# A sliding-window copy on one core: SP's copies shifted by two packets per DMA engine, the mends moved to ACT's queue

## The chip, the cores and the metric

The kernel runs on one core of one Trainium2 chip. Nothing is computed on the compute engines; every byte is moved by the core's 16 DMA engines, which take their work from three queues: SP's (q1 in the profile), ACT's (q10) and POOL's (q0). The metric is device time in microseconds (us), the median of several runs; lower is better.

## The reference

The input has 32 batches of 4096 rows of 256 floats. Each batch yields 127 windows of 64 rows, one every 32 rows:

```python
n_windows = (length - window_size) // stride + 1        # (4096 - 64)//32 + 1 = 127
for i in range(n_windows):
    start = i * stride
    result[:, i] = x[:, start:start + window_size].copy()
```

A *block* is 32 rows, 32 KB; a batch has 128 blocks. A *window* is two neighbouring blocks, 64 KB, so every inner block is written twice. The output is 32 x 127 windows, 266 MB.

## The kernel before

**Two ways for a batch.** The odd batches 1, 3, ..., 21 (`STAGED`, eleven of them, numbered n = 0 to 10) go through SBUF: a load of 4 MB puts block p on partition p of one of five tiles, and a store writes each block to its two places, 8 MB in packets of 32 KB. The loads are queued by POOL in packets of 16 KB (load 0 by ACT), the stores by ACT. All other batches go straight from DRAM to DRAM on SP's queue, one packet of 64 KB for each window (`rows`). A DMA of 128 rows gives each of the 16 engines 8 packets, one of 112 rows gives it 7, one of 32 rows 2; an instruction's packets are followed on each engine by a 4-byte packet that reports to the semaphore.

**Overruns and what mends them.** A store writes the halves from one before its batch to one after it, so it spoils the last half window of the batch before and the first half window of the batch behind. `full(b)` copies 128 windows of a batch that has 127, so it spoils window 0 of the next batch. Whatever is spoiled is written again later, and the order of these writes is what the waits guard:

- `EARLY` = 16, 18, 20, 22 are copied whole at the start (semaphore `early`), before the stores of 15 to 21, which wait for them. The halves that those stores spoil are rewritten by the two *mends* (`halves`, 48 and 64 packets of 2 KB), which wait for those stores.
- `ROW` = 24 to 30 are copied whole one after the other: each waits for the one before (`chain`), since each spoils the next one's window 0.
- `BESIDE` = 0, 2, ..., 14: windows 15 to 126 are copied after the store of batch b + 1 has landed; windows 0 to 14 come later, for four batches in one DMA (`firsts`, 60 packets of 64 KB).
- 23 and 31: their windows 15 to 126 come behind the loop (23 in two parts), windows 0 to 14 at the very end (`firsts((23, 31))`, 30 packets), when the copies of 22 and 30 have landed.

**SP's order.** Everything on SP's queue is written out by hand in `copies()` and `ends()`. At the start there are four copies: 48 windows of batch 16 (in packets of 32 KB, L136), its other 80, and two of 64 windows of batch 18. Then the loop over `BESIDE` alternates one whole batch (20, 22, 24, ..., 29: 128 windows) with 112 windows of a `BESIDE` batch. One passage through the loop is 240 packets of 64 KB on SP's queue, and it stands against one store (256 packets of 32 KB) and one load (256 of 16 KB). Behind the loop come `firsts` of 0 to 6, batch 30, then 32 and 80 windows of 23 and 112 of 31, then (after waits for `early`, for `fringe` and for three stores) the mends, `firsts` of 8 to 14 and `firsts` of 23 and 31.

**ACT's order.** Load 0, stores 0 to 9, and the last store in three pieces (`LAST`): blocks 0 to 31, blocks 96 to 127 (both report to `fringe`) and blocks 32 to 95.

**POOL** queues loads 1 to 10, each waiting for the store that frees its tile, and at the end waits for every semaphore. All DMA instructions carry line L84, the helper `start`.

Of the kernel before, what the change touches and what calls it, by code (L numbers as in the profile page):

```python
# [16 lines left out]
EARLY = (16, 18, 20, 22)  # L17
ROW = tuple(range(24, 31))
BESIDE = tuple(range(0, 16, 2))

REST = 15
# [5 lines left out]
class _Geometry:  # L27


    def __init__(self, x, out, W, S):  # L30
        self.B, self.L, self.D = x.shape
        self.x, self.out = x, out
        self.n_win = (self.L - W) // S + 1
        self.n_blk = self.L // S
        self.blk = S * self.D
        self.win = W * self.D
        assert W == 2 * S and self.n_blk == self.n_win + 1 == 128
# [33 lines left out]
class _Kernel:  # L71
    def __init__(self, nc, g, tiles):
        self.nc, self.g, self.tiles = nc, g, tiles
        self.loaded = [nc.alloc_semaphore(f"loaded{i}") for i in range(len(tiles))]
        self.stored = [nc.alloc_semaphore(f"stored{i}") for i in range(len(tiles))]
        self.copied = nc.alloc_semaphore("copied")
        self.chain = nc.alloc_semaphore("chain")
        self.first = nc.alloc_semaphore("first")
        self.early = nc.alloc_semaphore("early")
        self.fringe = nc.alloc_semaphore("fringe")  # L80
        self.count = {}

    def start(self, engine, out, in_, sem, packet=65536):
# [46 lines left out]
    def copies(self):  # L130


        g, nc, n_win = self.g, self.nc, self.g.n_win
        sp = nc.sync

        self.rows(EARLY[0], 0, 48, self.early, COPY_PACKET // 2)  # L136
        self.rows(EARLY[0], 48, 80, self.early)
        self.rows(EARLY[1], 0, 64, self.early)
        self.rows(EARLY[1], 64, 64, self.early)

        whole = EARLY[2:] + ROW
        for n, b in enumerate(BESIDE):
            if whole[n] in ROW[1:]:
                self.all_of(sp, self.chain)
            self.full(whole[n], self.early if whole[n] in EARLY else self.chain)
            self.after_store(sp, STAGED.index(b + 1))
            self.rows(b, REST, n_win - REST, self.copied)

        self.start(sp, *g.firsts(BESIDE[:4]), self.copied)
        self.all_of(sp, self.chain)  # L150
        self.full(ROW[-1], self.chain)
        self.rows(23, REST, 32, self.copied)

    def ends(self):
        g, nc, n_win = self.g, self.nc, self.g.n_win
        sp = nc.sync

        self.rows(23, REST + 32, n_win - REST - 32, self.copied)
        self.rows(31, REST, n_win - REST, self.copied)
        self.all_of(sp, self.early)  # L160
        self.all_of(sp, self.fringe)
        for n, s in enumerate(STAGED[:-1]):
            if s + 1 in EARLY:
                self.after_store(sp, n)
        self.start(sp, *g.halves(EARLY[:3], 2 * n_win - 1, g.n_blk - 1), self.copied)
        self.start(sp, *g.halves(EARLY, 0, 0), self.copied)
        self.start(sp, *g.firsts(BESIDE[4:]), self.copied)
        self.all_of(sp, self.chain)
        self.start(sp, *g.firsts((23, 31)), self.copied)


@with_exitstack
def kernel(
    ctx: ExitStack,
    tc: tile.TileContext,
    x: bass.AP,
    window_size: bass.AP,
    stride: bass.AP,
    out: bass.AP,
):  # L180
    nc = tc.nc
    W, S = int(window_size), int(stride)
    g = _Geometry(x, out, W, S)
    assert 0 not in STAGED and g.B - 1 not in STAGED
    pool = ctx.enter_context(tc.tile_pool(name="blocks", bufs=1))
    tiles = [pool.tile([g.n_blk, g.blk], x.dtype, name=f"xb{i}") for i in range(BUFS)]

    with tc.tile_critical():
        k = _Kernel(nc, g, tiles)
        k.load(0)  # L190
        k.copies()
        for n in range(1, len(STAGED)):
            k.load(n)
        waited = False
        last = len(STAGED) - 1
        for n, s in enumerate(STAGED):
            if not waited and (s - 1 in EARLY or s + 1 in EARLY):
                k.all_of(nc.scalar, k.early)
                waited = True
            if n < last:  # L200
                k.store(n, 0, g.n_blk)
            else:
                for p0, rows in LAST:
                    alone = p0 > 0 and p0 + rows < g.n_blk
                    k.store(n, p0, rows, None if alone else k.fringe)

        k.ends()

        sems = [*k.loaded, *k.stored, k.first, k.early, k.copied, k.chain, k.fringe]
        for sem in sems:  # L210
            k.all_of(nc.gpsimd, sem)
        nc.gpsimd.dma_reset()
        used = sorted(sem.num for sem in sems)
        assert used == list(range(used[0], used[-1] + 1))
        nc.gpsimd.sem_clear(range(used[0], used[-1] + 1))
# [35 lines left out]
```

## Time and profile before

| | |
|---|---|
| median of 3 runs | 766.52 us (763.76 to 766.72) |
| the profiled execution | 766.23 us, of it span 764.5 us |
| moved by the DMA engines | 314.15 MB, mean 411 GB/s |
| read from and written to HBM | 221.87 MB and 268.01 MB, 641 GB/s over the span |
| SP's queue q1 | 175.74 MB |
| ACT's queue q10 | 96.47 MB |
| POOL's queue q0 | 41.94 MB |
| an 8 MB store of ACT, from issue to landing (median) | 102.8 us |
| the mends, from issue to landing | 7.4 us (96 KB) and 11.5 us (128 KB) |
| last instructions of SP's queue issued | 732.82 to 738.45 us |

The three queues' bytes count every packet once; a packet from DRAM to DRAM is read from and written to HBM, a load is only read, a store only written. A queue's *share* in the profile is the time that its packets took, added up over the 16 engines and divided by 16 times the stretch asked for. So share x 16 x stretch / packets is the time of one packet. "Under 512 B" counts mostly the 4-byte reports to semaphores.

### The profile page before, as it was taken

What the parts mean: (1) busy time and instruction counts of PE and PEld (TensorE: products, weight loads), DVE (VectorE), ACT (ScalarE), POOL (GpSimd) and SP (SyncE); (2) the same over time, 40 slices, a digit from 0 to 9 for tenths busy, and PEclk for the clock granted to TensorE, in tenths of its full rate; (3) what the DMA queues carried; (4) which work ended last, traced back from release to release, by engine and by line L of the source; (5) the groups of instructions that cost most, each with busy time, mean ns of one, the idle gap of its engine ahead of it and who ended that gap; (6) DMA issues with size and microseconds to landing.
All of it is one profiled execution on the core that took longest, in us unless ns stands there. A gap on an engine that the chain in (4) does not pass through costs nothing.

```text
span 764.5 us, 116 instructions
## 1 busy us (share of the span) xinstructions
POOL 7.5 (1%) x14
## 2 busy tenths in 40 slices
POOL 1000000000000000000000000000000000000000
DMA  9999999999999999999999999999999999999995
GB/s 375 434 421 410 415 441 413 424 393 436 412 423 420 432 409 413 435 414 430 393 427 422 412 426 426 428 399 424 421 418 425 402 421 413 424 407 394 393 420 192
DMA packets 9187, 314.15 MB, mean 411 GB/s; under 512 B 845, under 2 KB 845, under 8 KB 957
## 3 DMA queue, kind: packets, MB, share of 16 engines
q1 hardware_dynamic: 3299, 175.74, 55.9%
q10 hardware_dynamic: 3168, 96.47, 30.0%
q0 software_dynamic: 2720, 41.94, 13.1%
HBM read 221.87 MB, written 268.01 MB: 641 GB/s over the span
## 4 chain that ended last, share of the span: by engine, by line
another core or an unknown queue 56%; POOL 1%; issue 0%; PEldq 0%
POOL xb L84 1%; PEldq L246 0%
## 5 line engine op out<-in xcount | busy, mean ns | idle before, releaser
L84 POOL DMA_DIRECT2D xb<-in_x_dram x10 | 7.3, 728 | 430.9 <-DMA out_dram<-xb 429.9
L232 POOL MEMSET const-bfloat16-1.0<- 128x1 bf16 x1 | 0.1, 96 | 0.0
L232 POOL MEMSET const-float32-0.0<- 128x1 f32 x1 | 0.1, 93 | 0.2 <-issue 0.2
L232 POOL MEMSET const-uint8-127<- 128x1 uint8 x1 | 0.1, 94 | 0.0
L232 POOL MEMSET const-float32-1.0<- 128x1 f32 x1 | 0.1, 93 | 0.0
## 6 DMA issues: line engine op xcount, KB each, us to landing
out_dram<-xb ACTq DMA_DIRECT2D x10, 8192.0 KB, 102.8
xb<-in_x_dram POOLq DMA_DIRECT2D x10, 4096.0 KB, 236.7
xb<-in_x_dram ACTq DMA_DIRECT2D x1, 4096.0 KB, 23.2
out_dram<-xb ACTq DMA_DIRECT2D x2, 2048.0 KB, 52.7
out_dram<-xb ACTq DMA_DIRECT2D x1, 4096.0 KB, 70.5
out_dram<-in_x_dram SPq DMA_DIRECT2D x1, 3072.0 KB, 23.8
out_dram<-in_x_dram SPq DMA_DIRECT2D x26, 67.6
out_dram<-in_x_dram SPq DMA_DIRECT2D x1, 128.0 KB, 11.5
```

What stands on the lines that cost most here:

```text
L84: engine.dma_start(out=out, in_=in_, max_dma_last_dim=packet).then_inc(sem, 16)
L232: nc = _bacc.Bacc("TRN2", target_bir_lowering=False, num_devices=1)
```

## The change

`copies()` now copies batch 18 in one DMA of 128 windows instead of two of 64, and adds 32 windows of batch 23 (15 to 46) right behind it, ahead of the loop. The loop itself is untouched. Behind it, 23's windows 47 to 78 stand where 15 to 46 stood; then come 31's 112 windows, the last 48 of 23, `firsts` of 8 to 14, the waits for `early` and `chain`, and `firsts` of 23 and 31. SP no longer waits for stores behind the loop, and `ends()` is gone. The two mends, with their waits for `fringe` and for the three stores, are issued by ACT behind its last store (`mends()`), on a semaphore of their own, `mended`.

```diff
-        self.rows(EARLY[1], 0, 64, self.early)
-        self.rows(EARLY[1], 64, 64, self.early)
+        self.full(EARLY[1], self.early)
+        self.rows(23, REST, 32, self.copied)
...
         self.full(ROW[-1], self.chain)
-        self.rows(23, REST, 32, self.copied)
-
-    def ends(self):
-        g, nc, n_win = self.g, self.nc, self.g.n_win
-        sp = nc.sync
-
-        self.rows(23, REST + 32, n_win - REST - 32, self.copied)
+        self.rows(23, REST + 32, 32, self.copied)
+
         self.rows(31, REST, n_win - REST, self.copied)
+        self.rows(23, REST + 64, n_win - REST - 64, self.copied)
+        self.start(sp, *g.firsts(BESIDE[4:]), self.copied)
         self.all_of(sp, self.early)
-        self.all_of(sp, self.fringe)
+        self.all_of(sp, self.chain)
+        self.start(sp, *g.firsts((23, 31)), self.copied)
+
+    def mends(self):
+
+        g, act = self.g, self.nc.scalar
+        self.all_of(act, self.fringe)
         for n, s in enumerate(STAGED[:-1]):
             if s + 1 in EARLY:
-                self.after_store(sp, n)
-        self.start(sp, *g.halves(EARLY[:3], 2 * n_win - 1, g.n_blk - 1), self.copied)
-        self.start(sp, *g.halves(EARLY, 0, 0), self.copied)
-        self.start(sp, *g.firsts(BESIDE[4:]), self.copied)
-        self.all_of(sp, self.chain)
-        self.start(sp, *g.firsts((23, 31)), self.copied)
+                self.after_store(act, n)
+        self.start(act, *g.halves(EARLY[:3], 2 * g.n_win - 1, g.n_blk - 1), self.mended)
+        self.start(act, *g.halves(EARLY, 0, 0), self.mended)
```

More of the change, by code (lines that the diff above doesn't have):

```diff
@@ L80, in __init__ @@
         self.fringe = nc.alloc_semaphore("fringe")
+        self.mended = nc.alloc_semaphore("mended")
         self.count = {}
@@ L205 @@
                     k.store(n, p0, rows, None if alone else k.fringe)
-        k.ends()
-        sems = [*k.loaded, *k.stored, k.first, k.early, k.copied, k.chain, k.fringe]
+        k.mends()
+        sems = [*k.loaded, *k.stored, k.first, k.early, k.copied, k.chain, k.fringe, k.mended]
         for sem in sems:
```

## The prediction

> **What bounds the kernel now.** I read the page first, then the DMA queues in short stretches, then the landings and the single packets of one engine.
>
> ```profile
> DMA  9999999999999999999999999999999999999995
> q1 hardware_dynamic: 3299, 175.74, 55.9%
> q10 hardware_dynamic: 3168, 96.47, 30.0%
> q0 software_dynamic: 2720, 41.94, 13.1%
> ```
>
> The engines are busy throughout: 55.9 + 30.0 + 13.1 = 99.0%. No wait of an instruction sets the end; the sum of packet times does. All that can be won is packets that take less than now and the 1% of idle time (7.6 us) at the two ends. POOL's 430 us of waiting costs nothing.
>
> So: how long is a packet? SP's 64 KB take 55.9% x 764.5 x 16 / (175.74 MB / 65,536) = 2.55 us on average. Three stretches around the end of one store of ACT, which lands at 437.6, in this order: 416 to 428, 428 to 438, 438 to 448 us.
>
> ```profile
> q1 hardware_dynamic: 56, 2.62, 50.5%
> q10 hardware_dynamic: 55, 1.67, 32.2%
> ...
> q1 hardware_dynamic: 37, 2.42, 64.8%
> q10 hardware_dynamic: 38, 0.85, 19.8%
> q0 software_dynamic: 36, 0.59, 15.1%
> ...
> q1 hardware_dynamic: 38, 2.49, 57.5%
> q10 hardware_dynamic: 37, 1.21, 28.1%
> ```
>
> First stretch: 50.5% x 12 x 16 / 40.0 packets = 2.42 us. Second: 64.8% x 160 / 36.9 = 2.81. Third: 57.5% x 160 / 38.0 = 2.42. The middle one is where a store gives way to the next on ACT's queue: q10 falls to 0.85 MB, and SP fills the gap. In the first stretch SP changes from one copy to the next (its share falls to 50.5%), and no packet suffers.
>
> Why that is, one engine's packets between 350 and 372 us show (S = SP 64 KB, A = ACT 32 KB, P = POOL 16 KB, s and a = their semaphore reports of 0.01 us): P s A P S A P S **a** P S A P S. The queues take turns, one packet each, and a report uses up a turn. Where ACT's turn is a report, two S stand with only a P between them: they took 2.42 and then 2.74 us, and the next 3.01. On nearly every engine one of the two S behind a takes 2.7 to 3.8 us. Where SP's turn is a report, A, P, A stand side by side: nothing is slow.
>
> SP's report comes two rounds before ACT's. A passage of SP's loop is 8 + 1 + 7 + 1 = 17 turns; a store is 16 + 1 and a load 16 + 1. All three recur every 17 rounds, so the distance stays: a `BESIDE` copy issued at 437.59 lands 58.3 us later at 495.9, the store issued at 402.94 lands 102.6 later at 505.5, 9.6 us apart; at 301.4 it is 9.1, at 573.6 it is 9.8.
>
> Last, the end: 674 to 728, 732 to 740 and 744 to 756 us.
>
> ```profile
> q1 hardware_dynamic: 264, 14.16, 66.5%
> q10 hardware_dynamic: 265, 7.41, 34.3%
> ...
> q10 hardware_dynamic: 92, 2.75, 79.7%
> q1 hardware_dynamic: 100, 0.60, 21.1%
> ...
> q1 hardware_dynamic: 85, 3.88, 91.7%
> ```
>
> Without POOL the 64 KB take 2.66 us; then ACT runs almost alone beside the 2 KB mends; then SP alone at 2.97 us a packet.
>
> **The change part by part.** *The shift.* Behind the copy of 48 windows SP had 6 + 5 + 5 = 16 turns ahead of the loop (80, 64 and 64 windows, each with a report); now it has 6 + 9 + 3 = 18 (80, 128 and 32). The loop begins two turns later, and SP's report falls into the round of ACT's: S A P **s a** P S A P. No two S have a lone P between them. This holds at every store, since each recurs in 17 turns, if SP's queue never runs dry. It doesn't: a `BESIDE` copy is issued when a store lands (437.59) while a whole batch of some 36 us still stands in the queue, now 8.5 us more of it than before; a whole batch is issued when the one before has landed (464.42), with a `BESIDE` copy of 31 us ahead of it, as before.
>
> *What a store's end costs now.* In the ten us before a landing, each queue's (packet time - 2.42, 1.21 or 0.61) x packets / 16: at 437.6 SP 0.39 x 36.9 / 16 = 0.90, POOL (0.67 - 0.61) x 36 / 16 = 0.13: 1.03 us. The same rows give 0.91, 1.23, 0.91, 1.03, 1.16, 1.00, 1.07, 1.06 and 0.88 for the nine landings from 96 to 642: 9.25 us together. Not all of it comes back as time. SP's old report stretch, free of excess now, becomes an ordinary one: between store ends the excess is 1.18 us in 55.5 (mean of six periods), and as some 11 of these are the free stretch, 0.027 a us, 0.27 for ten us, 2.4 for nine. Shift: -9.25 + 2.4 = -6.8 us. The bounds: nothing, if the excess only moves; -9.25, if the new stretch gives the same relief. I take -6.8, because the relief stretch (2.42 us with SP at its report) and the kernel's start show the packets next to such a round: at 23 to 27 us, with ACT's queue empty and SP's report between two P, P s P S, the S took 2.42.
>
> *The mends.* On SP they are 3 + 4 packets and two reports an engine, in turns with ACT's 32 KB (7.4 and 11.5 us to landing). Their packets total 112 x 0.09 / 16 = 0.65 us. The waits for `fringe` and the stores move to ACT, behind its last instruction: nothing but the mends is queued behind them there, and POOL's final wait, which gets one semaphore more (0.09 us). `fringe` is complete at 732.8, when the last piece of 8 packets an engine is still running, so ACT's queue has no gap.
>
> *The end.* Behind store 9 SP has 8 + 4 + 5 + 3 = 20 turns, ACT 5 + 5 + 9 = 19 and then the mends: both end in about the same round. Compare per engine from the landing of 31 before (726.7 to 736.3, about 731.5), with 6 S and 7 or 8 A left. Before: 7.5 x 1.21 + 0.65 + 6 x 2.93 (746 to 762 us) = 27.3. After, side by side at the packet times of 674 to 732 (2.65 and 1.30): 15.9 + 9.75 + 0.65 = 26.3. -1.0 us. Bounds: +2 (the engines end 6.4 us apart now; the slowest decides, and mends alone at the end may not be hidden) to -3.
>
> *The rest* (one DMA issue fewer at the start, four waits of SP) lies beside busy queues: nothing; if that cover were gone, an issue is 0.5 to 0.9 us.
>
> Sum: 766.2 (profiled execution; 0.3 below the median of 766.5) - 6.8 - 1.0 = 758.4, and 0.3 more against the median: **758.7 us**.
>
> **The rivals.** *The excess only moves (22%).* HBM delivers 641 GB/s over the span, and a period of 68.2 us (store landings 96.0 to 641.9, eight periods) moves 16 x (2 x 15 x 64 + 16 x 32 + 16 x 16 KB) = 44.0 MB, 645 GB/s; without any excess it would be 15 x 2.42 + 16 x 1.21 + 16 x 0.61 = 65.4 us. If memory and not the sequence is the limit, packets elsewhere grow by what the store ends lose, and only the end is won: 765.5. For it: 674 to 732 us, two queues, is slow at every packet. Against it: 416 to 428 and 438 to 448 show 436 and 431 GB/s without excess, and 428 to 438 only 387. The Trainium skill (DMA: Bandwidth & Descriptors, Rules for kernel authors) speaks for this rival: spreading DMAs over SP, ACT and GpSimd doesn't help bandwidth, as they interleave on the same 16 engines. By that rule the sum would be that of the rival or 766.5; the trace's 2.42 against 2.81 us speaks against it, as far as it is read to mean that the order of interleaving is free.
>
> *Both queues restart together (12%, slower).* In the shared round an engine has only two 16 KB loads in flight, and SP and ACT start cold side by side. Price by the dearest rows: the kernel's first 33 packets of ACT (1.9 to 5 us, 102.6%, 1.54 us each) cost 0.33 x 33 / 16 = 0.68, SP's first of 64 KB (24 to 30 us, 93.4%, 2.80 each) 0.38 x 32 / 16 = 0.76: 1.44 a store end, in place of 1.03 and with the 0.27: nine times 0.68 is +6.1, less 1.0: 771.6. It eats up all gain from about 0.9 us a store end, and costs 0.5% from 1.3. Against it: P s P S at 23 us shows no slow packet.
>
> *The distance isn't two everywhere (6%).* If ACT's store 0 enters its turns one round later in another execution, SP's report precedes ACT's by one, and S a P S stays: 765.5.
>
> **How the numbers follow.** The forecast has 60%, with 754 to 763 of its own. 0.5% is 3.8 us, about what can be told from no change. Faster, below 762.7: the forecast nearly whole and a little of the first rival, 0.60. Same: the first and last rivals and the forecast's edge, 0.28. Slower, above 770.4: the restart, 0.12. The range 754 to 767 holds the forecast and the two rivals at 765.5 and leaves out the restart and the far edge.
>
> **What would show it.** Right: the ten us before a store's landing show q1 at about 2.45 us a packet and q10 at about 1.1 MB instead of 0.85; a `BESIDE` copy lands within 2 us of a store; q1's share falls from 55.9% of 764.5 (427 us) to about 421 us; mends the last to land, within 2 us of SP's last copy. Wrong: the same landings together but 2.55 us a packet on average (it moved), or packets of over 2.8 us right behind the common landing (restart), or landings still 4 us apart.

## The result, and the profile after

The changed kernel takes 762.04 us (median of 6, 758.98 to 762.37) against 766.08 us (median of 6): ratio 0.994, 95% interval 0.9926 to 0.9954. The profiled execution is one of the quicker ones, 760.51 us with a span of 758.7. On two other chips the same pair gave 0.9913 (0.9897 to 0.993) and 0.9919 (0.9891 to 0.9947). It is faster: by 4.0 us on the first chip, about half of the 7.8 that were forecast.

From the page of the changed kernel, the busy row of the DMA engines and the three queues:

```profile
DMA  9999999999999999999999999999999999999996
q1 hardware_dynamic: 3155, 175.51, 55.3%
q10 hardware_dynamic: 3312, 96.70, 30.7%
q0 software_dynamic: 2720, 41.94, 13.3%
```

55.3 + 30.7 + 13.3 = 99.3% of 758.7 us is 753.4 us of packets for each engine, against 756.9 before: 3.5 us by these rounded shares, 3.8 by the single packet records. The 112 packets of the mends have gone from q1 to q10, with their 32 reports.

The placing is as forecast. Issues and landings of the changed kernel: a store issued at 403.50 (first line), a `BESIDE` copy issued at 436.10 (second):

```profile
out_dram<-xb ACTq DMA_DIRECT2D x1, 8192.0 KB, 100.2
out_dram<-in_x_dram SPq DMA_DIRECT2D x1, 67.4
```

403.50 + 100.2 = 503.7 and 436.10 + 67.4 = 503.5: 0.2 us apart where it was 9.6. The single packets of an engine there read S A P s a P S A P S, both reports in one round.

The DMA queues around a store's end (landing at 436.1), 428 to 438 us, and then the stretch up to the next, 438 to 490:

```profile
q1 hardware_dynamic: 52, 2.42, 56.4%
q10 hardware_dynamic: 50, 1.15, 26.7%
q0 software_dynamic: 50, 0.82, 19.1%
...
q1 hardware_dynamic: 200, 12.06, 55.1%
q10 hardware_dynamic: 202, 6.62, 30.6%
```

At the store's end a 64 KB packet takes 56.4% x 160 / 36.9 = 2.44 us; it was 2.81. But between store ends it takes 55.1% x 832 / 184.0 = 2.49, and ACT's 32 KB take 30.6% x 832 / 202 = 1.26. Before, the like stretch (440 to 492 us) reads:

```profile
q1 hardware_dynamic: 213, 11.93, 54.0%
q10 hardware_dynamic: 213, 6.98, 31.6%
```

2.47 and 1.23 us. So the packets between have grown. (Part of this is that the earlier stretch holds 31 of SP's reports and the later one 16: the report of the `BESIDE` copy, with its relief, has moved to the store's end.)

The end of the changed kernel, 728 to 752 us:

```profile
q1 hardware_dynamic: 121, 5.90, 58.0%
q10 hardware_dynamic: 160, 3.86, 38.4%
```

SP and ACT run side by side until the end, SP's packets at 58.0% x 384 / 90.0 = 2.47 us; before, SP was alone at 2.97. The last landings are 756.8 (ACT's last store), 757.0 (SP) and 757.3 us (the mends); before it was 762.9.

**The whole account**, from the packet records of both traces. The excess of a packet is its time over 2.418, 1.212 or 0.611 us (64, 32, 16 KB), summed and divided by 16 engines. A store end reaches from 1 us ahead of its landing on the first engine to 2 us behind that on the last; nine of them (stores 0 to 8) and the eight stretches between:

| excess, us an engine | before | after |
|---|---|---|
| nine store ends | 9.4 | 1.3 |
| the stretches between them | 10.2 | 16.3 |
| from 730 us on | 2.5 | 0.5 |
| the rest | 8.1 | 8.4 |
| engines idle until the last landing | 6.0 | 4.3 |

Store ends -8.1, between +6.1, end -2.0, idle -1.7, the rest +0.3: -5.5 us (unrounded), which is the last landing, 762.9 to 757.3. Three quarters of what the store ends lost came back between them.

A single landing would have misled here. The last engine of store 8 landed 3.8 us earlier (641.9 to 638.1), the first one 1.0 us later (629.1 to 630.1); the account goes by the mean of the 16 engines.

### The profile page after: what moved, and what is told of

Its sections match the earlier page's. It is cut to its first block, busy times and chain, and to the rows that moved or that the text cites. A ratio compares the mean times of both kernels' runs of the same rounds, so it can differ in the third digit from the quotient of the medians.

```text
span 758.7 us, 118 instructions
## 1 busy us (share of the span) xinstructions
POOL 7.4 (1%) x14
## 3 DMA queue, kind: packets, MB, share of 16 engines
q1 hardware_dynamic: 3155, 175.51, 55.3%
q10 hardware_dynamic: 3312, 96.70, 30.7%
q0 software_dynamic: 2720, 41.94, 13.3%
## 4 chain that ended last, share of the span: by engine, by line
another core or an unknown queue 56%; POOL 1%; issue 0%; PEldq 0%
POOL xb L85 1%; PEldq L247 0%
```

## The experiments

Chip A is that of the result (766 us for the kernel before). Three groups of four kernels ran on three other chips, B, C and D, which took 756 us for the kernel before. Ratios are to the kernel before on the same chip; times that an expectation gives for a chip of 766 us are compared as ratios. "Store ends" and "between" are excess in us an engine, over nine store ends and the eight stretches between them, as in the table above. A round is one turn of each queue.

**The parts alone (chip B).** `shift_only` keeps the old end:

```diff
-        self.rows(EARLY[1], 0, 64, self.early)
-        self.rows(EARLY[1], 64, 64, self.early)
+        self.full(EARLY[1], self.early)
+        self.rows(23, REST, 32, self.copied)
...
         self.full(ROW[-1], self.chain)
-        self.rows(23, REST, 32, self.copied)
```

> The shift of two turns alone; the mends and the order of the end stay as before. Two theories. A, the sequence: the store ends are made cheap (from 1.03 us each to about 0.2) and most of it is won, store 8 lands near 638 us instead of 642, and the time is about 762.5, nearly all of the change's gain. B, the excess moves: store ends are as cheap, but the stretches between them go from 1.2 us of excess to 1.9, the mean of the engines gains 1.6 us, and the time is 764.5 or more; the gain of the whole change comes from its end.

751.11 us, ratio 0.9944 (0.9931 to 0.9957).

`end_only` is the changed kernel with the old start:

```diff
-        self.full(EARLY[1], self.early)
-        self.rows(23, REST, 32, self.copied)
+        self.rows(EARLY[1], 0, 64, self.early)
+        self.rows(EARLY[1], 64, 64, self.early)
...
-        self.rows(23, REST + 32, 32, self.copied)
+        self.rows(23, REST, 64, self.copied)
```

> The new end alone (mends behind ACT's last store, SP's last copies without a gap); batch 18 is copied in two halves and nothing of 23 is copied early, so SP's report stays two turns ahead of ACT's. A: store ends still cost 1.03 us each, the end gives 1.0 to 1.7 us, time about 765. B: the end gives what the whole change gives, packets 2.0 us and less idle time 1.7 us, time about 762.3.

754.49 us, ratio 0.9982 (0.9969 to 0.9994). On this chip the shift is the larger part by far, as A had it: store ends 7.8 us in `end_only`, 0.4 in `shift_only`. But between them the excess is 3.5 in the one and 6.3 in the other: B's mechanism is there too, with 2.8 of 7.4 us coming back. As ratios to 766.1 us, A's times (762.5 and 765: 0.995 and 0.999) lie in both intervals, B's (764.5 and 762.3: 0.998 and 0.995) in neither; what A had left out is what comes back. The product of the ratios is 0.9926, near the changed kernel's.

**One and three turns of shift (chip B).** In the changed kernel:

```diff
-        self.rows(23, REST, 32, self.copied)
+        self.rows(23, REST, 16, self.copied)
...
-        self.rows(23, REST + 32, 32, self.copied)
+        self.rows(23, REST + 16, 48, self.copied)
```

and likewise 48 and then 16 windows for three turns (`shift3`).

> The changed kernel with one turn of shift (16 windows of 23 early) instead of two. SP's report comes in the round ahead of ACT's, and ACT's report again stands between two 64 KB packets with only one 16 KB load. A: store ends cost about 1 us each as before, time about 765 to 766, as with the end alone. B: the sequence is paid for elsewhere, time within 1 us of the changed kernel, 762 to 763.

752.06 us, ratio 0.9954 (0.9939 to 0.9968).

> The changed kernel with three turns of shift (48 windows of 23 early). SP's report comes one round behind ACT's, so that between two 64 KB packets there always stand at least a 32 KB and a 16 KB packet, but the two reports don't share a round. A: store ends as cheap as in the changed kernel (0.2 us), time 762, within 1 us. If it is the shared round that matters and not the sequence, store ends cost 0.5 us or more and the time is 764 or more. B: within 1 us of the changed kernel whatever the store ends cost.

749.07 us, ratio 0.9917 (0.9903 to 0.9931). With one turn the packets read s A P S a P S: the sequence that I had called dear is there. The queues of `shift1`, 416.5 to 426.5 us, a store landing at 426.5:

```profile
q1 hardware_dynamic: 53, 2.42, 59.3%
q10 hardware_dynamic: 50, 1.11, 25.9%
```

That is 2.57 us a packet, and this is the dearest of the nine, 0.52 us; the others cost 0.07 to 0.37. All nine together cost 1.9 us, against 7.8 in `end_only`, where each cost 0.59 to 1.30. A had said about 9. Two 64 KB packets with only a 16 KB one between are cheap if SP's own report came just a round earlier. So A's reason falls, although the shift itself pays.

**Before, after, three and four turns (chip C).**

> The kernel before, for a profile on the same chip as the next three. The last four kernels ran on a chip on which it took 756 us and not 766. If the chips differ in what memory gives, this profile shows the stretches between store ends (1.27 us of excess each on the first chip) at 0.4 to 0.6 us on a chip that takes 756, and the store ends at about 1 us on either.

756.07 us in one execution. Store ends 6.8 us, between them 3.9; on chip A it was 9.4 and 10.2. So the chips do differ, most of all in the stretches between.

> The changed kernel on the same chip as the others. If the parts add up, its ratio to the kernel before is 0.9944 x 0.9982 = 0.993 on a chip of 756 us; store ends 0.05 to 0.15 us each, and the stretches between them dearer by 0.3 us than in the kernel before there (0.7 us on a chip of 766).

749.25 us, ratio 0.9913 (0.9897 to 0.993). Store ends 0.6, between 6.2: 2.3 of the 6.2 us came back.

> Three turns of shift beside two, on one chip. With 0.9917 measured for it, it should be 0.1% to 0.3% faster than the changed kernel if SP's report behind ACT's is better than in the same round; equal if the difference was that of the runs.

749.12 us, ratio 0.9908 (0.9891 to 0.9925): no difference from the changed kernel that these runs can tell. Store ends 0.2, between 6.6. Three turns are no better version.

The edit of `shift4` is the one above with 64 windows early and none there.

> Four turns of shift (64 windows of 23 early): SP's report comes two rounds behind ACT's, the mirror image of the kernel before. Theory A, the sequence: ACT's report stands between two 64 KB packets again, and store ends cost 0.8 to 1.0 us each; ratio to the kernel before about 0.998, as with the end alone. Theory C, the demand on memory over some rounds: what helps is a report of SP close to that of ACT, on whichever side; with one round ahead a store end cost 0.2 us although the sequence was the dear one; two rounds behind then costs about as much as two rounds ahead, less what the neighbours' reports relieve, 0.5 to 1.0 us, and the ratio is 0.995 to 0.998. If it is as cheap as three turns (below 0.1 us), order matters: the report must not come ahead.

755.31 us, ratio 0.9989 (0.9978 to 0.9999). Store ends 5.8 us, between 4.6. The mirror image is nearly as dear as the original. On the chips of 756 us, with SP's report at -2, -1, 0, +1 and +2 rounds from ACT's, the nine store ends cost 6.8 to 8.0, 1.9, 0.4 to 1.2, 0.2 to 0.3 and 5.8 us: a report of SP within a round of ACT's, on either side, makes up for it. Theory C fits this, the demand on memory over a few rounds: on each engine a round without ACT's 32 KB asks memory for (2 x 64 + 16) KB in 3.03 us (779 GB/s over 16 engines), where a full one asks for 176 KB in 4.24 (680), and a round without SP's 64 KB for 48 KB in 1.82 (431). C's store ends, 0.5 to 1.0 us each, came (0.64 on average); its ratio, 0.995 to 0.998, did not, and A's 0.998 was nearer.

**The demand lowered (chip D).** POOL's loads read a fixed tile in SBUF:

```diff
-        src = g.src(STAGED[n], 0, [[g.blk, g.n_blk], [1, g.blk]])
...
+            src = bass.AP(fr.tensor, fr.offset, [list(fr.ap[0]), [0, 2], [1, half]])
```

> The kernel before, with POOL's ten loads taken from a fixed tile in SBUF (filled once by a DMA of 2 MB) instead of from DRAM: packets, turns and order as before, but a round asks 160 KB of memory and not 176. It leaves out the loading of the batches, so the odd batches' output is that of the tile. Theory A, the sequence: two 64 KB packets with only a 16 KB one between them stay as dear as they are, store ends about 0.7 to 1 us each. Theory C, the demand on memory over some rounds: store ends fall to 0.2 us or less each and the stretches between them to near nothing (below 0.1 us); store 8 lands about 9 us earlier on a chip of 756.

749.67 us in one execution. The second takes the same edit in the changed kernel.

> The same with the changed kernel's order. Theory C: with the demand down there is nothing left for the shift to win in the loop, and store 8 lands within 1 us of the run before this one; the end is still 2 to 4 us shorter. Theory A: store ends are cheap here and dear there, and store 8 lands 6 to 8 us earlier here.

745.05 us in one execution. The packets read S a P S in both. SP's report comes four or five rounds behind ACT's in the first and two or three ahead in the second, since the fill of the tile at the start moved the queues by some turns. So neither has the distance of the kernel that it was made from. `light_before`, 417.6 to 427.6 us, a store landing at 427.6:

```profile
q1 hardware_dynamic: 47, 3.08, 71.0%
q10 hardware_dynamic: 47, 1.02, 23.6%
```

71.0% x 160 / 47.0 = 2.42 us: the dear sequence without any excess. Over nine store ends it is 0.2 us, between them 1.3, and 0.2 and 0.3 in `light_after`. Store 8 lands at 620.9 and 623.5 us: with the demand down, the order of the reports is worth nothing that these two executions show. The last landing is still 4.5 us earlier (746.2 to 741.8), 2.5 of it from 730 us on and idle time. Theory C had this, though store 8 was to land within 1 us and came 2.6 us later, and its 9 us against the kernel before were 12.4 (633.2 in `before_c`); A had 6 to 8 us between the two. What stays untested is the shared round itself with the demand down. The two pages side by side with that of the kernel before on the same chip (`before_c`, then `light_before`):

```profile
HBM read 221.87 MB, written 268.01 MB: 649 GB/s over the span
...
HBM read 182.03 MB, written 268.01 MB: 602 GB/s over the span
```

The packet records show why "over a few rounds" matters. Take slices of 4 us around a store's end (mean of stores 2 to 8), and as demand what the packets would have moved without excess. `light_before` asks for some 615 GB/s in ordinary rounds and for 711 in the slice of the peak, and no slice has an excess over 0.7% of its time. `before_b` asks for 680 and for 742, with 2.3% in ordinary rounds and 9.9% in the slice behind the peak. So 711 GB/s for 4 us is not dear where the rounds around it leave room.

> The kernel before once more, for a profile on the chip of the next three. If this chip takes 766 us, the stretches between store ends should show some 10 us of excess in all, as on the first chip; if it takes 756, some 4 us.

757.09 us in one execution; store ends 8.0, between 4.6.

> The changed kernel again. If the chip decides how much of the store ends' gain comes back between them, its ratio is about 0.991 on a chip of 756 us (2.3 us come back) and about 0.994 on one of 766 us (6.1 us come back).

749.99 us, ratio 0.9919 (0.9891 to 0.9947); store ends 1.2, between 7.7: 3.0 of 6.8 us came back. As expected for a chip of 756. (The profiled execution was the slowest of the six, 755.26 us: one engine went on alone for some 4.5 us at the end, which counts as idle time of the others and not as excess.) No further chip of 766 us was met: that the chip decides the share rests on one chip against two, and the intervals of the ratios (0.9926 to 0.9954 on A, 0.9897 to 0.993 and 0.9891 to 0.9947 on C and D) overlap.

## Why the prediction was right, and where it was not

- **What bounds the kernel**: right. The end moved by the sum of packet times (3.8 us of excess) and idle time (1.7), and by no wait.
- **The shift puts the two reports in one round**: right, 0.2 us apart at the stores landing from 95 to 571 us, and SP's queue never ran dry.
- **Store ends become cheap**: right, 9.4 to 1.3 us. The forecast had 9.25 to zero, with 2.4 coming back. The signs that were named for "right" all came (2.44 us and 1.15 MB at the store's end, landings together, q1 at 55.3% of 758.7 = 420 us, the mends within 0.4 us of SP's last copy), but none of them looks at the stretches between, where the forecast failed.
- **What comes back**: this is the term that was mis-sized. 2.4 us were forecast and 6.1 measured on chip A; the loop gained 2.0 us and not 6.8. On chips C and D 2.3 and 3.0 us came back and the loop gained 3.9 and 3.8. I had worked it out from the stretches as they were, at 0.027 us a us, and that rate itself rose (on A from 1.27 to 2.0 us for each stretch). Two causes are likely, and no run separates them: the two relief places became one, and what the store ends took is asked of memory elsewhere.
- **The reason for it**, two 64 KB packets with a lone 16 KB packet between, was wrong: `shift1` has that order at a quarter of its price, and `light_before` without any. What is dear, as far as the runs show, is a few rounds together in which the engines ask memory for more than it gives. The S of 2.42 us at 23 to 27 us, on which I had leaned, stood behind a time of low demand, rounds of (2 x 32 + 32 + 16) KB in 3.03 us (605 GB/s); the very next S took 3.0 to 3.3 us on every engine, which I had not read. And the 436, 387 and 431 GB/s that I had held against the memory count a copy once: through memory the same rows give 653, 628 and 680 GB/s. That memory passed less at the store's end than beside it, where some 700 were asked, is more than a fixed ceiling explains; why is open.
- **The rival "the excess only moves"** had the better mechanism, and on A three quarters of it happened. In full it is refuted: it left nothing of the store ends' gain, and in ratio the shift alone is worth 0.56% on chip B. The Trainium skill (HBM Reference, Specifications) puts the memory at about 716 GB/s for a pair of cores; the trace fits it: in 744 to 756 us of the kernel before, SP alone moved 3.88 MB, twice that through memory in 12 us, 647 GB/s, with packets 2.97 us instead of 2.42.
- **Spreading over queues**: the Trainium skill's rule that it doesn't help (DMA: Bandwidth & Descriptors, Rules for kernel authors) is about how many queues are used, which no run here varies; for their phase the runs show 0.8% (three turns against four, 0.9908 and 0.9989 on chip C, with the same bytes on the same queues).
- **The end**: -1.0 us forecast, -3.7 measured (2.0 of packets, 1.7 of idle time). I had priced SP's last packets by the stretch from 674 to 732 us, 2.65 us; they took 2.47, on fifteen engines. And I had left idle time out of the sum: both queues now end together on each engine. The mends alone at the end cost some 0.6 us on an engine, as forecast; the last of them lands 0.4 us behind SP.
- **The restart** didn't come: the packet behind the shared round took 2.42 us on nearly every engine.

Two errors of opposite sign, +4.8 in the loop and -2.7 at the end, met in part and left 2.1 us; the median execution was 1.5 us slower than the profiled one, where 0.3 had been allowed. That is how 758.7 became 762.0. That the time still fell into the forecast's own 754 to 763 us was luck: without the 2.7 us that the end gave beyond its forecast it would have been 764.7, nearer to the first rival's 765.5.

## What to carry to other kernels

When every DMA engine is busy, look at the time of one packet, stretch by stretch: share x stretch x 16 / packets. Where it rises, ask what the queues together demand of memory there and in the few rounds around it, and let the light turns of one queue (its reports, its small packets) fall where another queue's light turns leave only the heavy packets. Count as won only the part that isn't asked for again a few rounds later, and let all queues end together.

## What the runs showed that was not expected

- The same kernel takes 766 us on one chip and 756 on three others. The difference lies in the excess (30.3 us an engine on A, 19.3 on C), most of it between store ends (10.2 against 3.9); 64 KB packets without excess take 2.418 us on both. Why a chip gives less is open.
- A report of 4 bytes takes 0.01 us and still a whole turn of its queue: 17 turns for 16 packets. The Trainium skill (DMA: Bandwidth & Descriptors, Queues, rings and completion order) has engines change between queues by packets of some 9 to 17 descriptors; here each turn was one packet of the trace, of 64 KB, 2 KB or 4 bytes.
- One engine gets nothing of the three `firsts` copies, whose outer count is 15, and is done at 739.6 us before and 737.7 after, some 20 us ahead of the others.
